# Full 128x128 stationaries for every matmul of the attentions and the decays

## The chip, the cores and the metric

The kernel runs on one core of a Trainium2 chip. The metric is the device time of one execution in microseconds, the median of the runs of the same kernel.

## The reference, cut to what matters

Two transformer blocks are computed one after the other on a sequence of 256 positions of width 1024, in float32. Three parts matter here.

The first block has a stick-breaking attention with 8 heads of 64 columns. For the scores z = q.k/8 of one head, a strictly causal mask, and s before t, the weight is sigmoid(z[t,s]) times the product of (1 - sigmoid(z[t,j])) over s < j < t. The output is the weights times the values.

The second block has a gated delta rule with 8 heads of 128 columns in chunks of 64 positions. It needs two masked matrices of decays exp(G[c] - G[s]) for each head, one with the diagonal and one without, multiplied into the products q.k and k.k.

Beside it stands a forgetting attention, a causal softmax attention with 8 heads of 128 columns, to whose scores cum[t] - cum[s] is added, where cum is the running sum of the log forget gates.

## The kernel before, in words

Positions are split into two tiles of 128. Large projections (`proj_T`, L237) stream their weights from HBM in pieces of 512 KB; ScalarE rounds a piece to f32r (`wh`, L192), VectorE makes the rest (`wl`, L193), and TensorE multiplies the rounded weights with the activation's two halves (L232, 512 columns a pass) and the rests with its upper half (L234, 256 columns). ScalarE and VectorE add the two halves of a result into SBUF (L245, L246). `proj_N512` does the same with positions on the output's partitions (L270 to L272).

The small attention steps are threaded into these projections: generators stand in a list `late`, and `tick()` (called in every column tile of a projection) advances the first of them at a set pace. `piped` runs three heads staggered, each with one of its three steps. The order of instructions on each engine is then worked out by a planner, from priorities and from when operands are expected to be ready; it is not written out by hand.

A matmul's stationary operand is loaded by an instruction of its own (PEld in the profile). An f32 matmul is two passes, an f32r matmul one.

In `att_head` (L500) a mask is laid into a PSUM bank by an identity times `mstrict` (L505, 384 columns: two triangles with zeros between them), and the scores are added: L506 and L507 have 64 rows of `kT` as their stationary, since a head is 64 partitions of a tile that holds two heads. The second step multiplies by triangles of minus ones (L518, L519). The third multiplies the weights with 64 columns of the values `vN` (L525, L526) into 64 partitions of the bank.

In `gdn_products` (L906) each head gets a mask by an identity times `mgdn` (L914, 512 columns), and the sums of the log decays by a matmul whose stationary is a column of `selc` repeated, on 40 rows (L915); the rows `o.rows` hold the sums of 8 heads at partitions 0 to 7 and the rests of their rounding at 32 to 39. Then come the products of queries and keys (L922, L923).

In `fox_head` (L1097) it is the same with `mfox` (L1101), the rows `frows` on 40 partitions (L1102), and the scores (L1105), which have full stationaries, as have the values of this attention (L1130, L1131).

The masks are built on GpSimd at the start of the program. The delta rule's substitution runs on GpSimd later (L935 to L952), beside the projections of the forgetting attention, and its results are loaded by L962 for the matmuls from L971 on.

Of the kernel before, what the change touches and what calls it, by code (L numbers as in the profile page):

```python
# [11 lines left out]
F32 = mybir.dt.float32  # L12
# [6 lines left out]
P = 128  # L19
# [20 lines left out]
def two_blocks(ctx, tc, ins, out):  # L40
# [16 lines left out]
    def nm(s):  # L57
        cnt[0] += 1
        return f"{s}_{cnt[0]}"

    def t4(s, shape=(P, 4, T), dt=F32):
        return p4.tile(list(shape), dt, tag="t4", name=nm(s))
# [73 lines left out]
    def sel(dst, op, fill, base, cm, pattern):  # L136
        nc.gpsimd.affine_select(out=dst, in_=dst, compare_op=op, fill=fill, base=base,
                                pattern=pattern, channel_multiplier=cm)
# [305 lines left out]
        mm_N(pv[tt], wrow[k], k, h, k, tt, slice(None), k == 0, k == KD - 1)  # L444
    for tt in range(NT):
        nc.scalar.copy(vN[:, tt, :], pv[tt])
    qT, kT = t4("qT"), t4("kT")
    for j, pt in proj_T(w_in, 0, ATT_W, h):
        nc.scalar.activation(qT[:, j:j + 2, :], pt, AF.Copy, scale=HEAD_DIM ** -0.5)
    for _ in proj_T(w_in, ATT_W, ATT_W, h, into([kT])):  # L450
        pass

# [9 lines left out]

    mtmp = t2("mtmp")

    mstrict = const.tile([P, 384], F32R, tag="mstrict", name="mstrict")
    nc.gpsimd.memset(mtmp, 0.0)
    sel(mtmp[:, 0:128], ALU.is_gt, -BIG, 0, -1, [[1, P]])
    sel(mtmp[:, 256:384], ALU.is_gt, -BIG, 0, -1, [[1, P]])
    nc.gpsimd.tensor_copy(mstrict, mtmp[:, 0:384])
    def row_tile(n, tag):  # L470
        return t1(tag, (n, P))

# [28 lines left out]
    def att_head(hp, hh):  # L501
        hd = 2 * hp + hh
        rows = slice(hh * 64, (hh + 1) * 64)
        pz = ps("pz")
        mm(pz[:, 0:384], ident_r, mstrict, start=True, stop=True)  # L505
        mm(pz[:, 0:256], kT[rows, hp, 0:P], qT[rows, hp, :], start=False, stop=True, skip_group_check=True)  # L506
        mm(pz[:, 256:384], kT[rows, hp, P:T], qT[rows, hp, P:T], start=False, stop=True, skip_group_check=True)  # L507
        la = ta("la")
        nc.scalar.activation(la[:, 0:384], pz[:, 0:384], AF.Abs)
        nc.scalar.activation(la[:, 0:384], la[:, 0:384], AF.Exp, scale=-1.0)  # L510
        nc.scalar.activation(la[:, 0:384], la[:, 0:384], AF.Ln, bias=1.0)
        nc.vector.scalar_tensor_tensor(la[:, 0:384], pz[:, 0:384], 0.0, la[:, 0:384], ALU.max, ALU.add)
        sr = tc4("sr", (P, 2, 512), F32R)
        nc.scalar.copy(sr[:, 0, 0:384], la[:, 0:384])
        nc.vector.tensor_tensor(sr[:, 1, 0:384], la[:, 0:384], sr[:, 0, 0:384], op=ALU.subtract)
        yield
        for q in range(2):
            mm(pz[:, 0:384], nsuf_r, sr[:, q, 0:384], start=False, stop=True, skip_group_check=True)  # L518
            mm(pz[:, P:T], nones_r, sr[:, q, 256:384], start=False, stop=True, skip_group_check=True)  # L519
        wgt = la  # L520
        nc.scalar.activation(wgt[:, 0:384], pz[:, 0:384], AF.Exp)
        yield
        cs = slice(hd * 64, (hd + 1) * 64)
        po = pz[rows, 0:T]
        mm(po, vN[:, 0, cs], wgt[:, 0:256], start=True, stop=True)  # L525
        mm(po[:, P:T], vN[:, 1, cs], wgt[:, 256:384], start=False, stop=True, skip_group_check=True)  # L526
        hi, lo = oh.at(hp)
        split(hi[rows], lo[rows], po)

    def piped(gens):  # L530

# [23 lines left out]


    mtmp2 = t2("mtmp2")
    mfox = const.tile([P, 384], F32R, tag="mfox", name="mfox")
    nc.gpsimd.memset(mtmp2, 0.0)
    sel(mtmp2[:, 0:128], ALU.is_ge, -BIG, 0, 1, [[-1, P]])  # L560
    sel(mtmp2[:, 256:384], ALU.is_ge, -BIG, 0, 1, [[-1, P]])
    nc.gpsimd.tensor_copy(mfox, mtmp2[:, 0:384])

    mtmp3 = t2("mtmp3")
    mgdn = const.tile([P, 512], F32R, tag="mgdn", name="mgdn")
    nc.gpsimd.memset(mtmp3, 0.0)
    for a in range(4):
        o = a * P
        sel(mtmp3[:, o:o + P], ALU.is_ge if a < 2 else ALU.is_gt, -BIG, 0, -1, [[1, P]])
    nc.gpsimd.tensor_copy(mgdn, mtmp3)  # L570
    zero = const.tile([P, 160], F32, tag="zero", name="zero")
    nc.gpsimd.memset(zero, 0.0)

    selt = const.tile([40, 8], F32, tag="selt", name="selt")
    nc.gpsimd.memset(selt, 0.0)
    for q in (0, 32):
        nc.gpsimd.memset(selt[q:q + 8], 1.0)
        sel(selt[q:q + 8], ALU.is_equal, 0.0, 0, 1, [[-1, 8]])
    selc = const.tile([40, 8], F32R, tag="selc", name="selc")
    nc.gpsimd.tensor_copy(selc, selt)  # L580

    bias24 = const.tile([P, 24], F32, tag="bias24", name="bias24")
# [192 lines left out]
    def gate_sums():  # L775

        pG = ps("pG")
        pGt = pG[:, 0:80].rearrange("p (t c) -> p t c", t=NT)
        mm(pGt[:, :, 24:32], ctr, vals[:, :, 0:8], start=True, stop=True)
        mm(pGt[:, :, 32:40], suf, vals[:, :, 0:8], start=True, stop=True)  # L780
        mm(pGt[:, :, 0:24], tri, vals, start=True, stop=True)
        mm(pGt[:, 1, 16:24], ones, vals[:, 0, 16:24], start=False, stop=True, skip_group_check=True)
        nc.vector.tensor_copy(Gs, pGt)
        nc.vector.tensor_scalar(sl2, Gs[:, :, 16:24], -1.0, None, ALU.mult)
        nc.scalar.activation(beta, vals[:, :, 8:16], AF.Exp)
        nc.scalar.activation(eG, Gs[:, :, 0:8], AF.Exp)
        nc.vector.tensor_scalar(hbeta, beta, 0.5, None, ALU.mult)
        pr_ = to_rows(sl2[:, :, None, :])

        frows = const.tile([40, 384], F32R, tag="frows", name="frows")  # L790
        nc.vector.tensor_copy(frows[:, 0:P], pr_[:, 0, 0:P])
        nc.vector.tensor_copy(frows[:, P:384], pr_[:, 0])
        return frows

    def sum_sq(dst, y):

# [87 lines left out]
    def gdn_decay(o):  # L884

        h0 = o.h0

        ln = tn("ln", (P, HG, NT))
        nc.scalar.activation(ln, o.sk, AF.Ln, bias=eps4)
        nc.vector.tensor_scalar(ln, ln, -0.5, None, ALU.mult)  # L890
        G, Gc, Gr = (Gs[:, :, k + h0:k + h0 + HG].rearrange("p t h -> p h t") for k in (0, 24, 32))
        lb = vals[:, :, 8 + h0:8 + h0 + HG].rearrange("p t h -> p h t")

        rv = tn("rv", (P, NT, 2, HG))
        rvv = rv.rearrange("p t a h -> p a h t")
        o.cv = pg1.tile([P, 3, HG, NT], F32, tag="cv", name=nm("cv"))
        nc.vector.tensor_add(o.cv[:, 1], ln, lb)
        nc.vector.tensor_copy(rvv[:, 0], Gc)
        nc.vector.tensor_add(rvv[:, 1], o.cv[:, 1], Gc)
        o.rows = p1.tile([40, 2, T], F32R, tag="rows", name=nm("rows"), bufs=1)  # L900
        nc.vector.tensor_copy(o.rows, to_rows(rv))

        nc.vector.tensor_sub(o.cv[:, 0], ln, Gc)
        nc.vector.tensor_add(o.cv[:, 1], o.cv[:, 1], G)
        nc.vector.tensor_add(o.cv[:, 2], ln, Gr)
        nc.scalar.activation(o.cv[:, 1:3], o.cv[:, 1:3], AF.Exp)  # L906

    def gdn_products(o):

        M = tc4("M", (P, HG, NT, P))  # L910
        o.At = tc4("At", (P, HG, NT, P))
        for hl in range(HG):
            pd = ps("pd", (P, 2, NT, P))
            mm(pd, ident_r, mgdn, start=True, stop=True)  # L914
            mm(pd, selc[:, hl:hl + 1].to_broadcast([40, P]), o.rows, start=False, stop=True, skip_group_check=True)  # L915
            ed = ta("ed", (P, 2, NT, P))
            for tt in range(NT):
                nc.scalar.activation(ed[:, :, tt, :], pd[:, :, tt, :], AF.Exp, bias=o.cv[:, 0, hl, tt:tt + 1])
            pk = ps("pk", (P, 2, NT, P))
            for tt in range(NT):  # L920
                xs = slice(tt * P, (tt + 1) * P)
                mm(pk[:, 0, tt, :], o.kT[:, hl, xs], o.qT[:, hl, xs], start=True, stop=True)  # L922
                mm(pk[:, 1, tt, :], o.kT[:, hl, xs], o.kT[:, hl, xs], start=True, stop=True)  # L923
            nc.vector.tensor_mul(M[:, hl], pk[:, 1], ed[:, 1])
            nc.vector.tensor_mul(o.At[:, hl], pk[:, 0], ed[:, 0])

        o.Mu = M.rearrange("p h t c -> p (h t) c")
        for b in range(4):
            bs = slice(b * 32, (b + 1) * 32)
            nc.sync.dma_start(scr[o.hg * UN:(o.hg + 1) * UN, b].rearrange("u r c -> r u c"), o.Mu[bs, :, bs])  # L930
# [166 lines left out]
    def fox_head(n, hl, qkT):  # L1097
        hd = n * HG + hl
        fq, fk = qkT[0][:, hl, :], qkT[1][:, hl, :]
        pz = ps("pz")  # L1100
        mm(pz[:, 0:384], ident_r, mfox, start=True, stop=True)  # L1101
        mm(pz[:, 0:384], selc[:, hd:hd + 1].to_broadcast([40, P]), frows, start=False, stop=True,  # L1102
           skip_group_check=True)
        for o, m, q0 in ((0, 1, 0), (128, 2, P)):
            mm(pz[:, o:o + m * P], fq[:, q0:q0 + P], fk[:, 0:m * P], start=False, stop=True,  # L1105
               skip_group_check=True)
# [37 lines left out]
                rests.pop(0)()  # L1144

    steps(gdn_k(g_[0]), 3)
    frows = gate_sums()
    steps(gdn_q(g_[0]), 3)
    g_.append(gdn_open(1))
    rests.append(lambda: gdn_decay(g_[0]))  # L1150
# [120 lines left out]
```

## Time and profile before

| what | value |
|---|---|
| median of 3 runs | 928.37 us (927.98 to 928.56) |
| profiled execution | 928.64 us, span 926.9 us |
| TensorE matmuls busy | 910.3 us (98%), 4891 |
| weight loads busy | 763.9 us (82%) |
| VectorE busy | 656.6 us (71%) |
| ScalarE busy | 571.5 us (62%) |
| GpSimd busy | 73.1 us (8%) |
| granted TensorE clock, mean | 0.998 of full speed |
| HBM read | 154.11 MB |

The span runs from the first to the last instruction of the profiled execution. Matmuls are pipelined and the ends of their records are modelled, so that a busy TensorE need not be at its peak; what a matmul adds to the end is better read in the chain of waits, where each piece reaches from the end of the piece before it to its own.

### The profile page before, as it was taken

The page shows a single profiled execution, that of the slowest core. Times are in us where ns is not written, and L with a number is a line of the kernel's source. Part 1 is how long each engine was busy: PE and PEld are TensorE (multiplying, and loading weights), DVE is VectorE, ACT ScalarE, POOL GpSimd, SP SyncE. Part 2 cuts the span into 40 slices and gives each one's busy share as a digit, 9 for nine tenths or more (in the row PEclk, how much of TensorE's full clock was granted, in tenths as well). Part 3 has the DMA queues.
Part 4 walks back from the last instruction along what each step waited for, and adds up shares of the span by engine and source line. Part 5 has one row for each costly group of instructions (what it writes and reads, how often), then busy time and mean ns, then how long its engine had stood idle before and what let it go on. Part 6 is the DMA issues. An engine that isn't in the chain of part 4 may idle for free.

```text
span 926.9 us, 13384 instructions
## 1 busy us (share of the span) xinstructions
PE 910.3 (98%) x4891; PEld 763.9 (82%) x4891; DVE 656.6 (71%) x1154; ACT 571.5 (62%) x990; POOL 73.1 (8%) x127
## 2 busy tenths in 40 slices
PE   8999999999999999999999999999999999999998
PEld 4887888778888888778888768888998788888886
DVE  6556656985988889857989878645688765555553
ACT  5567765565765666647867667754455466556662
POOL 4000000000000000000000189401000000000000
PEclk9999999999999999999999999999999999999999
DMA  7653457556565555663645344544336754556552
GB/s 251 198 171 94 137 173 236 168 184 218 178 207 168 191 187 193 206 192 118 200 138 151 106 130 141 166 138 128 112 120 234 261 168 150 188 176 197 173 168 99
DMA packets 118873, 157.86 MB, mean 170 GB/s; under 512 B 9829, under 2 KB 96088, under 8 KB 118808
## 3 DMA queue, kind: packets, MB, share of 16 engines
q1 hardware_dynamic: 117336, 153.08, 51.7%
q10 hardware_dynamic: 720, 2.62, 0.9%
q0 software_dynamic: 752, 1.31, 0.6%
q8 instruction: 38, 0.62, 0.3%
q14 instruction: 27, 0.22, 0.1%
HBM read 154.11 MB, written 2.88 MB: 169 GB/s over the span
## 4 chain that ended last, share of the span: by engine, by line
PE 82%; DVE 8%; DMA 5%; ACT 3%; issue 2%; SPq 0%; ACTq 0%; DVEq 0%
PE pT L232 30%; PE pT L234 15%; PE pN L271 5%; PE pN L270 5%; PE pN L272 5%; PE pM L270 4%; PE pM L271 4%; PE pM L272 4%; DVE wl L193 3%; PE pS L1006 2%; DMA raw<-in_w_out_dram 1%; ACT wh L192 1%; DMA raw<-in_w_down_dram 1%; DMA raw<-in_w_up_dram 1%; DMA raw<-in_w_in_dram 1%
## 5 line engine op out<-in xcount | busy, mean ns | idle before, releaser
L193 DVE TENSOR_TENSOR wl<-raw,wh 128x1024 fp32r<-128x1024 f32 (+1 forms) x283 | 346.3, 1231 | 98.7 <-PE pT L234 74.0
L192 ACT CAST wh<-raw 128x1024 fp32r<-128x1024 f32 (+1 forms) x283 | 290.7, 1047 | 101.4 <-PE pT L232 38.0
L232 PE MATMUL pT<-uT,wh 128*128 128x512 f32 x384 | 102.2, 402 | 0.0
L246 DVE TENSOR_TENSOR py<-py,pT 128x256 f32<-128x256 f32 x136 | 56.0, 417 | 54.5 <-ACT py L245 54.1
L245 ACT COPY py<-pT 128x256 f32<-128x256 f32 x136 | 49.0, 369 | 60.2 <-PE pT L234 59.9
L270 PE MATMUL pN<-wh,fTh 128*128 128x512 f32 x216 | 84.1, 393 | 0.8 <-ACT wh L192 0.5
L271 PE MATMUL pN<-wl,fTh 128*128 128x512 f32 x216 | 84.2, 391 | 0.1
L272 PE MATMUL pN<-wh,fTl 128*128 128x512 f32 x216 | 83.8, 390 | 0.0
L232 PEld LDWEIGHTS pT<-uT,wh 128*128 128x128 f32 x384 | 68.5, 189 | 12.6 <-issue 0.5
L232 PE MATMUL pT<-hT,wh 128*128 128x512 f32 x288 | 73.4, 396 | 0.0
L232 PE MATMUL pT<-h2T,wh 128*128 128x512 f32 x288 | 72.2, 392 | 0.0
L232 PEld LDWEIGHTS pT<-hT,wh 128*128 128x128 f32 x288 | 51.6, 189 | 10.4 <-issue 0.2
L232 PEld LDWEIGHTS pT<-h2T,wh 128*128 128x128 f32 x288 | 52.1, 189 | 9.6
L234 PEld LDWEIGHTS pT<-uT,wl 128*128 128x128 f32 x384 | 52.3, 190 | 3.6
L234 PE MATMUL pT<-uT,wl 128*128 128x256 f32 x384 | 53.8, 283 | 0.0
L270 PEld LDWEIGHTS pN<-wh,fTh 128*128 128x128 f32 x216 | 40.5, 188 | 9.6 <-ACT wh L192 1.2
L232 PE MATMUL pT<-hnT,wh 128*128 128x512 f32 x192 | 47.8, 391 | 0.0
L271 PEld LDWEIGHTS pN<-wl,fTh 128*128 128x128 f32 x216 | 40.6, 188 | 8.4 <-DVE wl L193 0.5
L272 PEld LDWEIGHTS pN<-wh,fTl 128*128 128x128 f32 x216 | 40.6, 188 | 8.5
L234 PEld LDWEIGHTS pT<-hT,wl 128*128 128x128 f32 x288 | 39.3, 190 | 2.9
L234 PEld LDWEIGHTS pT<-h2T,wl 128*128 128x128 f32 x288 | 39.3, 190 | 2.8
L935 POOL DMA_DIRECT2D bm<-scr x1 | 0.8, 775 | 515.1 <-PE pM L271 515.1
(380 smaller groups left out, 1647.0 us busy)
## 6 DMA issues: line engine op xcount, KB each, us to landing
raw<-in_w_in_dram SPq DMA_DIRECT2D x111, 512.0 KB, 3.9
raw<-in_w_up_dram SPq DMA_DIRECT2D x76, 512.0 KB, 4.6
raw<-in_w_down_dram SPq DMA_DIRECT2D x54, 512.0 KB, 4.3
raw<-in_w_out_dram SPq DMA_DIRECT2D x16, 512.0 KB, 4.1
raw<-in_w_proj_fox_dram SPq DMA_DIRECT2D x8, 512.0 KB, 3.5
raw<-in_w_proj_gdn_dram SPq DMA_DIRECT2D x8, 512.0 KB, 4.2
raw<-in_w_att_branch_dram SPq DMA_DIRECT2D x4, 512.0 KB, 5.0
raw<-in_w_conv_branch_dram SPq DMA_DIRECT2D x4, 512.0 KB, 4.1
```

The source lines that it names most:

```text
L192: nc.scalar.copy(wh, raw)
L193: nc.vector.tensor_sub(wl, raw, wh)
L232: mm(dst, wt.at(k, cs)[0], x.both(k), start=(k == 0), stop=(k == kt - 1), skip_group_check=True)
L234: mm(dst[:, T:2 * T], wt.at(k, cs)[1], x.at(k)[0], start=False, stop=(k == kt - 1), skip_group_check=True)
L245: nc.scalar.copy(y[:, i, :], pt[:, 0:T])
L246: nc.vector.tensor_add(y[:, i, :], y[:, i, :], pt[:, T:2 * T])
L270: mm(dst, xh, wh, start=first, stop=False)
L271: mm(dst, xh, wl, start=False, stop=False)
L272: mm(dst, xl, wh, start=False, stop=last)
L935: nc.gpsimd.dma_start(bm, scr.rearrange("u b r c -> (u b) r c"))
L1006: mm(pt[:, hl, :], *f(hl), start=True, stop=True)
```

## The change

Every matmul of these three parts gets a stationary of 128 rows and 128 columns. The scaled queries of the first attention go into tiles in which the other head's 64 rows are zero, so that all 128 rows of `kT` can be the stationary. Its values are multiplied for both heads at once, and the half that belongs to the head is read out. The rows of sums (`grows`, `frows`) and `selc` are extended from 40 to 128 partitions with zeros; the two groups of heads share `grows`. The masks hold one triangle each, which the moving operand repeats (`diagonal`); where the mask was zero, nothing is written. In a forgetting head the rows of sums now come first and the mask second.

```diff
-    qT, kT = t4("qT"), t4("kT")
+    qz, kT = [tc4("qz", (P, 2, 2, T)) for _ in range(2)], t4("kT")
+    for q_ in qz:
+        for hh in range(2):
+            nc.gpsimd.memset(q_[(1 - hh) * 64:(2 - hh) * 64, :, hh, :], 0.0)
     for j, pt in proj_T(w_in, 0, ATT_W, h):
-        nc.scalar.activation(qT[:, j:j + 2, :], pt, AF.Copy, scale=HEAD_DIM ** -0.5)
+        for hh in range(2):
+            rows = slice(hh * 64, (hh + 1) * 64)
+            nc.scalar.activation(qz[j // 2][rows, :, hh, :], pt[rows], AF.Copy, scale=HEAD_DIM ** -0.5)
...
-    mstrict = const.tile([P, 384], F32R, tag="mstrict", name="mstrict")
+    mstrict = const.tile([P, P], F32R, tag="mstrict", name="mstrict")
...
+    def diagonal(pz, mask, start):
+
+        mm(pz.rearrange("p (b c) -> p b c", b=2)[:, :, 0:P], ident_r, mask[:, None, :].to_broadcast([P, 2, P]),
+           start=start, stop=True, skip_group_check=True)
...
-        mm(pz[:, 0:384], ident_r, mstrict, start=True, stop=True)
-        mm(pz[:, 0:256], kT[rows, hp, 0:P], qT[rows, hp, :], start=False, stop=True, skip_group_check=True)
-        mm(pz[:, 256:384], kT[rows, hp, P:T], qT[rows, hp, P:T], start=False, stop=True, skip_group_check=True)
+        q_ = qz[hp // 2][:, hp % 2, hh, :]
+        diagonal(pz, mstrict, True)
+        mm(pz[:, 0:256], kT[:, hp, 0:P], q_, start=False, stop=True, skip_group_check=True)
+        mm(pz[:, 256:384], kT[:, hp, P:T], q_[:, P:T], start=False, stop=True, skip_group_check=True)
...
-        cs = slice(hd * 64, (hd + 1) * 64)
-        po = pz[rows, 0:T]
+        cs = slice(hp * P, (hp + 1) * P)
+        po = pz[:, 0:T]
         mm(po, vN[:, 0, cs], wgt[:, 0:256], start=True, stop=True)
         mm(po[:, P:T], vN[:, 1, cs], wgt[:, 256:384], start=False, stop=True, skip_group_check=True)
         hi, lo = oh.at(hp)
-        split(hi[rows], lo[rows], po)
+        split(hi[rows], lo[rows], po[rows])
...
+    grows = const.tile([P, 2, T], F32R, tag="grows", name="grows")
+    nc.gpsimd.tensor_copy(grows.rearrange("p a t -> p (a t)"), mtmp2)
+    frows = const.tile([P, 384], F32R, tag="frows", name="frows")
+    nc.gpsimd.tensor_copy(frows, mtmp2[:, 0:384])
...
-    mgdn = const.tile([P, 512], F32R, tag="mgdn", name="mgdn")
+    mgdn = const.tile([P, 2, P], F32R, tag="mgdn", name="mgdn")
...
-    selc = const.tile([40, 8], F32R, tag="selc", name="selc")
+    selc = const.tile([P, 8], F32R, tag="selc", name="selc")
...
-        o.rows = p1.tile([40, 2, T], F32R, tag="rows", name=nm("rows"), bufs=1)
-        nc.vector.tensor_copy(o.rows, to_rows(rv))
+        nc.vector.tensor_copy(grows[0:40], to_rows(rv))
...
-            mm(pd, ident_r, mgdn, start=True, stop=True)
-            mm(pd, selc[:, hl:hl + 1].to_broadcast([40, P]), o.rows, start=False, stop=True, skip_group_check=True)
+            mm(pd, ident_r, mgdn[:, :, None, :].to_broadcast([P, 2, NT, P]), start=True, stop=True)
+            mm(pd, selc[:, hl:hl + 1].to_broadcast([P, P]), grows, start=False, stop=True, skip_group_check=True)
...
-        mm(pz[:, 0:384], ident_r, mfox, start=True, stop=True)
-        mm(pz[:, 0:384], selc[:, hd:hd + 1].to_broadcast([40, P]), frows, start=False, stop=True,
-           skip_group_check=True)
+        mm(pz[:, 0:384], selc[:, hd:hd + 1].to_broadcast([P, P]), frows, start=True, stop=True)
+        diagonal(pz, mfox, False)
```

## Rows read from the trace of the kernel before

**Rows 1.** The page's chain of waits, summed by engine.

```profile
PE 82%; DVE 8%; DMA 5%; ACT 3%; issue 2%; SPq 0%; ACTq 0%; DVEq 0%
```

**Rows 2.** Busy us per engine in three stretches (PE, PEld, DVE, ACT, POOL), clock, DMA, GB/s.

```profile
49.00:120.00 71.00, 71.00 (x382) 57.67 (x381) 46.78 (x78) 51.18 (x93) 0.00 (x0) 1.00 0.42 128
476.00:523.00 47.00, 47.00 (x260) 38.04 (x259) 41.61 (x99) 33.51 (x74) 0.00 (x0) 1.00 0.37 115
540.00:563.00 23.00, 21.14 (x98) 15.78 (x96) 18.30 (x39) 15.62 (x44) 20.96 (x27) 1.00 0.40 122
```

**Rows 3.** The chain in order of time, stick-breaking heads: start us, us added, piece.

```profile
56.52 0.18 PE pz L518
...
57.27 0.63 PE pz L506 x2
57.89 0.22 PE pz L507 x2
58.11 2.05 PE pT L232 x8
...
61.11 1.84 PE pT L232 x8
...
63.90 0.58 PE pz L525 x2
...
64.70 0.37 PE pz L518
...
80.37 0.41 PE pz L507 x2
```

**Rows 4.** Timeline of TensorE, first forgetting head: start us, us, engine, line, operation, shapes.

```profile
540.56 0.39 PE L272 MATMUL pM<-wh,uT 128*128 128x512 f32 x1
540.57 0.19 PEld L1101 LDWEIGHTS pz<-mfox,ident_r 128*128 128x128 f32 x1
...
540.79 0.34 PE L1101 MATMUL pz<-mfox,ident_r 128*128 128x384 f32 x1
...
541.05 0.18 PEld L1102 LDWEIGHTS pz<-frows,selc 40*128 40x128 f32 x1 [0.30 <-issue]
```

**Rows 5.** The chain in order of time, forgetting heads.

```profile
557.75 0.17 PE pz L1101
557.92 0.36 PE pz L1102
...
558.65 0.66 PE pz L1105 x4
...
566.37 0.43 PE pz L1130 x2
...
586.10 0.85 PE pz L1105 x4
```

**Rows 6.** The chain in order of time, decays of the delta rule.

```profile
483.80 0.24 PE pd L914
484.03 0.43 PE pd L915
...
486.90 0.42 PE pk L922 x2
...
487.55 0.22 PE pk L922 x2
```

**Rows 7.** The chain in order of time, where the substitution's result is first used.

```profile
606.70 0.84 PE pY L971 x8
```

**Rows 8.** Line 449: duration of one in ns (shortest, median, longest), starts, shapes.

```profile
L449 ACT ACTIVATE qT<-py x2: 632/633/634, 33.5 to 39.1; 128x512 f32<-128x512 f32 x2
```

**Rows 9.** The chain in order of time, ahead of the first forgetting head's maximum.

```profile
540.77 2.77 DVE wl L193 x2
```

**Rows 10.** Timeline of GpSimd, loads of the substitution's result.

```profile
590.41 2.30 POOL L962 DMA_DIRECT2D X<-scT  x4 [0.29 <-POOL X L959]
```

**Rows 11.** The chain in order of time, at the branch projections.

```profile
146.06 5.57 DMA raw<-in_w_att_branch_dram
```

More of the change, by code (lines that the diff above doesn't have):

```diff
@@ L463, in two_blocks @@
     mtmp = t2("mtmp")
-    mstrict = const.tile([P, 384], F32R, tag="mstrict", name="mstrict")
[L466 to L469, printed above, removed]
+    mstrict = const.tile([P, P], F32R, tag="mstrict", name="mstrict")
+    nc.gpsimd.memset(mtmp[:, 0:P], 0.0)
+    sel(mtmp[:, 0:P], ALU.is_gt, -BIG, 0, -1, [[1, P]])
+    nc.gpsimd.tensor_copy(mstrict, mtmp[:, 0:P])
+    def diagonal(pz, mask, start):
+        mm(pz.rearrange("p (b c) -> p b c", b=2)[:, :, 0:P], ident_r, mask[:, None, :].to_broadcast([P, 2, P]),
+           start=start, stop=True, skip_group_check=True)
     def row_tile(n, tag):
@@ L557, in two_blocks @@
     mtmp2 = t2("mtmp2")
-    mfox = const.tile([P, 384], F32R, tag="mfox", name="mfox")
+    mfox = const.tile([P, P], F32R, tag="mfox", name="mfox")
     nc.gpsimd.memset(mtmp2, 0.0)
-    sel(mtmp2[:, 0:128], ALU.is_ge, -BIG, 0, 1, [[-1, P]])
-    sel(mtmp2[:, 256:384], ALU.is_ge, -BIG, 0, 1, [[-1, P]])
-    nc.gpsimd.tensor_copy(mfox, mtmp2[:, 0:384])
-    mtmp3 = t2("mtmp3")
-    mgdn = const.tile([P, 512], F32R, tag="mgdn", name="mgdn")
[L566 to L570, printed above, removed]
+    grows = const.tile([P, 2, T], F32R, tag="grows", name="grows")
+    nc.gpsimd.tensor_copy(grows.rearrange("p a t -> p (a t)"), mtmp2)
+    frows = const.tile([P, 384], F32R, tag="frows", name="frows")
+    nc.gpsimd.tensor_copy(frows, mtmp2[:, 0:384])
+    sel(mtmp2[:, 0:P], ALU.is_ge, -BIG, 0, 1, [[-1, P]])
+    nc.gpsimd.tensor_copy(mfox, mtmp2[:, 0:P])
+    mtmp3 = t2("mtmp3")
+    mgdn = const.tile([P, 2, P], F32R, tag="mgdn", name="mgdn")
+    nc.gpsimd.memset(mtmp3[:, 0:2 * P], 0.0)
+    for a in range(2):
+        sel(mtmp3[:, a * P:(a + 1) * P], ALU.is_gt if a else ALU.is_ge, -BIG, 0, -1, [[1, P]])
+    nc.gpsimd.tensor_copy(mgdn.rearrange("p a c -> p (a c)"), mtmp3[:, 0:2 * P])
     zero = const.tile([P, 160], F32, tag="zero", name="zero")
     nc.gpsimd.memset(zero, 0.0)
-    selt = const.tile([40, 8], F32, tag="selt", name="selt")
+    selt = const.tile([P, 8], F32, tag="selt", name="selt")
     nc.gpsimd.memset(selt, 0.0)
@@ L788, in gate_sums @@
         pr_ = to_rows(sl2[:, :, None, :])
[L790 to L793, printed above, removed]
+        nc.vector.tensor_copy(frows[0:40, 0:P], pr_[:, 0, 0:P])
+        nc.vector.tensor_copy(frows[0:40, P:384], pr_[:, 0])
     def sum_sq(dst, y):
@@ L1146, in two_blocks @@
     steps(gdn_k(g_[0]), 3)
-    frows = gate_sums()
+    gate_sums()
     steps(gdn_q(g_[0]), 3)
```

## The prediction

> **What bounds the kernel now.** First I read the chain of waits, summed by engine [rows 1]: TensorE holds 82% of it, VectorE 8%, the DMAs 5%. So time taken off TensorE is worth something where the chain runs on TensorE, and nothing where it runs elsewhere; the question has to be asked stage by stage. Next come the busy times of the stretches with edited matmuls [rows 2]. In 49 to 120 us (the stick-breaking heads, threaded into projections) TensorE is busy in every microsecond, VectorE 46.78 of 71.00 and ScalarE 51.18: room on both. In 476 to 523 (the decays of the delta rule) TensorE is again always busy, but VectorE is at 41.61 of 47.00, with 5.4 us left. In 540 to 563 (the first four forgetting heads) TensorE rests for 1.9 us of 23 and the chain runs on other engines.
>
> Then the chain in order of time, piece by piece; its second column is what each piece adds to the end. The reader is to compare equal work. A 384-column pass on a full stationary adds 0.18 us (L518), but 0.37 right after the 64-column stationaries of L525 and L526. Eight passes of a projection add 1.84, but 2.05 right after L507, whose stationary has 64 rows [rows 3]. Nothing is late there: the two columns of TensorE's instructions show why [rows 4]. The load of a full stationary (L1101) starts 0.01 us after the matmul ahead of it started and lies wholly beside it; the load of the 40-row one (L1102) starts 0.26 us after L1101's matmul did, with 0.30 us of idle loader ended by "issue", which is nobody's result. A change of the stationary's shape costs a pause, both going in and coming out.
>
> **The change part by part.** Everything is summed against the profiled execution, 928.64 us (span 926.9), which is 0.27 above the median of the three runs.
>
> *Stick-breaking, in.* The two passes of L506 add 0.63 us [rows 3]; two 256-column passes of a full f32 stationary, L1130, add 0.43 [rows 5]. So 0.20 a head, 8 heads: 1.6. The zero rows themselves cost nothing: columns set the length of a pass, and their number stays. *Out*, into a projection: 2.05 - 1.84 = 0.21, 8 times, with smaller ones among them: 1.6. In two heads other matmuls stand between L506 and L507, so that L507 pays its own way in (0.41 against 0.22 [rows 3]) and the matmul between pays a way out (0.20): 2 x 0.39 = 0.8.
>
> *Values.* L525's two passes add 0.58 against the 0.43 of L1130: 0.15, 8 times, 1.2. The way out, 0.37 - 0.18 = 0.19, 8 times: 1.5. Both heads' values make the stationary 128 columns wide, L1130's shape exactly. Sum for this attention: 1.6 + 1.6 + 0.8 + 1.2 + 1.5 = 6.7.
>
> *Decays.* L915 adds 0.43 where 512 columns on a full stationary, L914, add 0.24: 0.19. The pair of passes behind it adds 0.42 where the next pair adds 0.22: 0.20 [rows 6]. 8 x 0.39 = 3.1.
>
> *Forgetting heads.* L1102 adds 0.36 where L1101 with as many columns adds 0.17; the four passes of L1105 add 0.85 behind it and 0.66 where a full stationary comes first [rows 5]. 8 x 0.38 = 3.0.
>
> *Masks.* One triangle in two places is 256 columns and not 384. By L1101, 0.17 us for 384, the 128 saved are 0.057 us, in 16 heads 0.9. The repeated reading and the gap in the output are new; L971 reads and writes short strided pieces, eight passes in 0.84 us or 0.105 each [rows 7], no more than the 0.11 of a pass in L922's quick pair [rows 6], so I charge nothing and bound it by a loss of 0.1 us in each of 24 mask matmuls (2.4 us).
>
> *Moved and added work.* The scaled queries are written by four ScalarE instructions of 64 partitions and not two of 128. One of 128x512 takes 632 ns [rows 8]; if half the partitions take as long, ScalarE has 1.3 us more between 33 and 39 us, beside TensorE's projections; uncovered it is a loss of 1.3, if halves take half, none. GpSimd gains four fills and two copies and loses mask work, all of it before the heads need it. The order of the mask and the row matmul in a forgetting head is swapped, with one end. No DMA and no wait is added. Total taken off TensorE: 6.7 + 3.1 + 3.0 + 0.9 = 13.7 us.
>
> **What of it lies on the path.** The stick-breaking part, 6.7 + 0.45 = 7.15, all of it: TensorE is the chain from 49 to 120 and the other engines have 20 us of room [rows 2]. Of the decays, between 0 and 3.1: VectorE has 5.4 us of rest in that stretch, but it is spread, and its work follows TensorE's; I take 2.3, three quarters, nearest to the row that has the chain on TensorE throughout. Of the first four forgetting heads, between 0 and 1.75 (4 x 0.38 + 4 x 0.057): at 540.77 the chain leaves TensorE for 2.77 us of VectorE's weight conversion [rows 9], and TensorE has rest already [rows 2], so I take 0; VectorE and ScalarE are late next there. The last four heads are on a chain of TensorE pieces (the 0.85 of [rows 5] is one): 1.75. GpSimd's substitution does not become late: its last load is issued from 590.41 [rows 10], and what needs it starts at 606.70 [rows 7], while only the 3.5 us of the forgetting heads come off between. Forecast: 7.15 + 2.3 + 0 + 1.75 = 11.2; 928.64 - 11.2 = 917.4, and by the median 917.2. I say 917.2, with 915.9 to 918.7 as this case's own range.
>
> A rule of the Trainium skill speaks against the change: in "TensorE: Matmul & The Clock Gate", section "Part 3: Packing small matmuls", a weight load overlaps a running matmul only where their row groups differ. By it a full stationary could never load beside another, and the sum would turn into the loss of the last rival below; by the rows it does load beside one, and the sum stands.
>
> **The rivals.** *All of it is on the path.* If VectorE's queue keeps up in both doubtful stretches, 928.64 - 13.7 = 914.9. For it: the 5.4 us of rest. Against: the rest of TensorE in 540 to 563.
>
> *VectorE becomes the bound* from the decays to the first forgetting heads, and what TensorE saves there turns into its waiting for converted weights: 928.64 - 7.15 - 1.75 = 919.7. For it: VectorE at 41.61 of 47.00 and the handover at 540.77. Against: up to there no piece of the chain is VectorE's.
>
> *The first gain is given back* at 146.06, where the chain passes for 5.57 us through the DMA of the branch weights [rows 11]: if that stream can't come sooner, 7.15 is lost and 928.64 - 4.05 = 924.6 stays. Against: the DMAs are at 0.42 of their time in 49 to 120 [rows 2], and a load is issued when TensorE and the converters free a buffer, so it moves with them.
>
> *It doesn't do what it says:* the pauses belong to the switch between f32 and f32r, or to a first use of an operand, and stay. Then only the masks count: 928.64 - 0.9 = 927.7. Against: L1130 and the 0.66 of L1105 are f32 passes behind f32r or transposes, with no pause [rows 5].
>
> *Slower.* Full loads are exposed. The change makes 80 loads full (32 for the scores, 32 for the values, 16 rows of sums). If each stood in line with the passes for its 0.19 us [rows 4], that would be 15.2, and 928.64 - 11.2 + 15.2 = 932.6. It decides from 0.14 us a load on. Against: the load of L1101 beside a running matmul [rows 4]. The page named above has the mechanism; the trace disagrees with it for full stationaries.
>
> **How the numbers follow.** Forecast 50%; all on the path 15%; VectorE the bound 20%; given back 8%; pauses stay 4%; slower 3%. The first three hold 85%, and the unknown prices (1.3 for ScalarE, 2.4 for the masks' access) reach a little beyond 919.7: range 913.5 to 922. The order of instructions on each engine is worked out anew for a changed kernel, which may move a stage by a microsecond either way; the range has room for it. A difference under 0.2% (1.9 us) can't be told from none: faster 0.93, same 0.04, slower 0.03.
>
> **What would show it.** In the profile after: no "issue" idle ahead of the score, value and row-sum loads; L506's successor at 0.43 for two passes, the value passes likewise; eight projection passes behind them at 1.84; the decay's row matmul at 0.24 and the pair behind it at 0.22; masks at 0.11 to 0.12. The stretch of the stick-breaking heads should end some 7 us sooner, and TensorE's rest after the decays should grow by 1 to 3 us. Wrong would be: loads that start after their matmuls and not beside them; a chain that runs on VectorE in the decays; the 7 us present at 120 and gone by 200.

## The result and the profile after

The changed kernel takes 918.36 us (median of 4 runs, 916.61 to 919.42), the kernel before 928.17 in 4 runs beside it: the ratio is 0.9898, with a 95% interval of 0.9879 to 0.9918. The forecast was 917.2. 9.8 us came off where 11.2 were forecast. That it came so near is in part luck: by the table of stages below, 4.55 us of losses that were not forecast stand against 2.73 of gains that were not forecast either. The profiled execution took 919.42 us, its span 917.7.

The edited matmuls have new line numbers: in the stick-breaking heads the mask is L478, the scores L518 and L519, the suffix triangles L530 and L531, the values L538 and L539; in the decays the mask is L927, the rows L928, the products L935 and L936; in the forgetting heads the rows are L1114, the mask L478 again, the scores L1117.

First the page: busy time by engine, and the chain summed by engine (against [rows 1]).

```profile
PE 899.6 (98%) x4891; PEld 763.2 (83%) x4891; DVE 656.4 (72%) x1154; ACT 572.6 (62%) x992; POOL 74.1 (8%) x129
...
PE 80%; DVE 10%; ACT 3%; DMA 3%; issue 2%; POOL 1%; DVEq 0%; ACTq 0%; SPq 0%; POOLq 0%
```

TensorE still holds the chain, with 2 points fewer and VectorE with 2 more. Next the same three stretches of work as in [rows 2], cut where the trace of after starts and ends the same matmuls: busy us of PE, PEld, DVE, ACT and POOL, clock, DMA share, GB/s.

```profile
48.50:113.80 65.30, 65.01 (x382) 57.16 (x381) 46.17 (x78) 51.30 (x93) 0.00 (x0) 1.00 0.46 138
472.40:516.50 44.10, 44.10 (x260) 38.20 (x259) 41.15 (x98) 33.22 (x74) 0.00 (x0) 1.00 0.43 123
533.40:555.60 22.20, 19.59 (x100) 15.67 (x98) 17.89 (x39) 15.63 (x44) 20.24 (x26) 1.00 0.44 127
```

The 382 matmuls of the first stretch take 65.30 us where they took 71.00, and TensorE now has small rests among them (0.29 us). The decays still show none. Then the chain in order of time in the stick-breaking heads, start us, us added, piece (against [rows 3]).

```profile
62.53 0.43 PE pz L538 x2
...
63.19 0.17 PE pz L530
...
63.71 0.17 PE pz L478
63.88 0.43 PE pz L518 x2
...
64.53 1.85 PE pT L232 x8
```

Values 0.43 (before 0.58), scores 0.43 (0.63), the projection behind them 1.85 (2.05), the triangle behind the values 0.17 (0.37): each pause is gone. The timeline of the first forgetting head shows how (against [rows 4]).

```profile
533.95 0.39 PE L272 MATMUL pM<-wh,uT 128*128 128x512 f32 x1
533.95 0.19 PEld L1114 LDWEIGHTS pz<-frows,selc 128*128 128x128 f32 x1
...
534.17 0.33 PE L1114 MATMUL pz<-frows,selc 128*128 128x384 f32 x1
534.17 0.19 PEld L478 LDWEIGHTS pz<-mfox,ident_r 128*128 128x128 f32 x1
```

The load of the row matmul, late by 0.26 us when it had 40 rows, starts with the matmul ahead of it. The decays and the forgetting heads, chain in order of time (against [rows 6] and [rows 5]):

```profile
477.65 0.23 PE pd L927
477.89 0.23 PE pd L928
...
478.58 0.22 PE pk L935 x2
...
578.04 0.17 PE pz L1114
578.21 0.12 PE pz L478
578.33 0.66 PE pz L1117 x4
```

Rows 0.23 for 0.43, the first pair behind them 0.22 for 0.42, rows of a forgetting head 0.17 for 0.36, its scores 0.66 for 0.85.

**Where the time came from, stage by stage.** I take the start of the same matmul in two traces, named by its time in before, and subtract what the stage started with. Minus is a gain, in us.

| from, to (us of before) | forecast | after | after, again | gain loads moved |
|---|---|---|---|---|
| start to 26.7 | 0 | -0.47 | -1.94 | -0.86 |
| to 137.6, stick-breaking | -7.15 | -5.73 | -5.74 | -5.76 |
| to 211.3, branches, merge, norms | 0 | +2.62 | +1.06 | -0.87 |
| to 476.3 | 0 | +0.04 | -0.09 | +0.01 |
| to 529.7, decays | -2.3 | -3.00 | -3.03 | -3.04 |
| to 563.1, first four forgetting heads | 0 | -0.98 | -0.62 | -0.90 |
| to 606.5, last four | -1.75 | -1.28 | -0.70 | -1.28 |
| to 765.7 | 0 | -0.58 | -0.40 | -0.59 |

The columns behind "after" are experiments 5 and 6. The first stage has no part of the change; over all profiles it differs by up to 2.7 us, so its figure is left out of the readings. Two stages ask for a reason: the stick-breaking heads gave 1.4 less than forecast, and the stage behind them gave 2.62 back. For the first, the chain of after a little later shows who comes last, and the waits of TensorE's loader between 40 and 130 us show how often (engine, line, releaser: us in total, times, longest).

```profile
71.73 0.69 DVE cu L609
...
75.76 0.52 ACT sr L526
...
76.30 0.57 DVE sr L527
...
76.92 0.45 PE pz L530
```

```profile
PEld pz L530 <- ACT sr L526: 1.0, 2, 0.6
PEld pz L530 <- DVE sr L527: 0.6, 2, 0.3
```

In the middle heads the convolution branch's product (L609) and taps share VectorE with the head's logarithm part `sr`, and with TensorE faster `sr` is late: 0.45 for a triangle that takes 0.17 above. Some 20 us later the chain pays for two more:

```profile
97.58 0.39 PE pz L530
...
98.55 0.26 PE pz L530
```

For the second, ScalarE's waits between 134 and 160 us, and the issue and landing of the load it waited for, first in after and then in before.

```profile
ACT wh L192 <- DMA raw<-in_w_conv_branch_dram: 3.4, 1, 3.4
```

```profile
L176 SPq DMA_DIRECT2D raw<-in_w_conv_branch_dram x1: 368/368/368, 136.0 to 136.0; - x1
...
DMA to landing us min/median/max: 9.5/9.5/9.5
```

```profile
L176 SPq DMA_DIRECT2D raw<-in_w_conv_branch_dram x1: 368/368/368, 141.9 to 141.9; - x1
...
DMA to landing us min/median/max: 6.2/6.2/6.2
```

The branch weight is issued 5.9 us sooner than before, but lands in 9.5 us where it took 6.2. Right behind it, on ScalarE's queue, go the two gain loads of the coming norms (512 KB each), issued at 136.3 and 136.7 in after, 142.5 and 142.9 before. What the late weight passes on is seen further down the chain: VectorE's conversions (`wl`, L193) come later, so the buffer that the first piece of the next weight, `in_w_out`, is to fill comes free later, and the chain goes through that load, first in after and then in before.

```profile
150.18 1.15 DVE wl L193
...
151.38 4.70 DMA raw<-in_w_out_dram
```

```profile
156.17 4.33 DMA raw<-in_w_out_dram
```

Counted from the start of the last gate projection (131.40 in after, 137.60 in before), this load is issued 1.41 us later than before and takes 0.37 longer.

### The profile page after: what moved, and what is told of

It is laid out like the page before. It is cut to its first block, busy times and chain, and to the rows that moved or that the text cites. A ratio compares the mean times of both kernels' runs of the same rounds, so it can differ in the third digit from the quotient of the medians.

```text
span 917.7 us, 13382 instructions
## 1 busy us (share of the span) xinstructions
PE 899.6 (98%) x4891; PEld 763.2 (83%) x4891; DVE 656.4 (72%) x1154; ACT 572.6 (62%) x992; POOL 74.1 (8%) x129
## 3 DMA queue, kind: packets, MB, share of 16 engines
q10 hardware_dynamic: 720, 2.62, 0.9%
## 4 chain that ended last, share of the span: by engine, by line
PE 80%; DVE 10%; ACT 3%; DMA 3%; issue 2%; POOL 1%; DVEq 0%; ACTq 0%; SPq 0%; POOLq 0%
PE pT L232 29%; PE pT L234 15%; PE pN L270 5%; PE pN L271 5%; PE pN L272 5%; DVE wl L193 5%; PE pM L271 4%; PE pM L272 4%; PE pM L270 4%; PE pS L1019 2%; ACT wh L192 1%; DMA raw<-in_w_up_dram 1%; DMA raw<-in_w_out_dram 1%; DMA raw<-in_w_in_dram 1%; DVE py L246 1%
## 5 line engine op out<-in xcount | busy, mean ns | idle before, releaser
L193 DVE TENSOR_TENSOR wl<-raw,wh 128x1024 fp32r<-128x1024 f32 (+1 forms) x283 | 346.7, 1232 | 95.9 <-PE pT L234 71.0
L272 PE MATMUL pN<-wh,fTl 128*128 128x512 f32 x216 | 83.8, 390 | 0.0
L272 PEld LDWEIGHTS pN<-wh,fTl 128*128 128x128 f32 x216 | 40.6, 188 | 8.5
```

The source lines that it names most:

```text
L193: nc.vector.tensor_sub(wl, raw, wh)
L272: mm(dst, xl, wh, start=False, stop=last)
```

## The experiments

Four kernels make one part of the change each, two pairs test the stage that gave back, and three ask what else the pauses and waits allow. None leaves out part of the computation.

**1. Scores alone** (zero-filled queries, full stationary; values, rows and masks as before).

```
-        mm(pz[:, 0:256], kT[rows, hp, 0:P], qT[rows, hp, :], start=False, stop=True, skip_group_check=True)
...
+        q_ = qz[hp // 2][:, hp % 2, hh, :]
+        mm(pz[:, 0:256], kT[:, hp, 0:P], q_, start=False, stop=True, skip_group_check=True)
```

> The kernel before with one part of the change: the scores of the stick-breaking heads with zero rows beside the 64, nothing else. Theory (a pause of 0.2 us at each change of the stationary's shape): two 256-column score passes add 0.43 and not 0.63 us, the projection passes behind them 1.84 and not 2.05; by 120 us the trace is 3.2 to 4.0 us ahead of before; the total is 2 to 4 us lower, less what is given back between 155 and 205 us. Rival (the pause belongs to the switch between f32 and f32r): no row changes, total within 1 us.

Measured: 924.77 us (8 runs) to 927.34 (20), ratio 0.9968 [0.9954, 0.9982]. The stick-breaking stage gained 3.79 of the 4.0 of the forecast's terms; 0.71 was given back by 211 us. Its chain (values are L531, scores L512):

```profile
62.46 0.58 PE pz L531 x2
...
64.21 0.43 PE pz L512 x2
...
64.86 1.82 PE pT L232 x8
```

The scores and the projection behind them lose their pauses, the values keep theirs: a pause goes with the shape of its own stationary.

**2. Values alone.**

```
-        cs = slice(hd * 64, (hd + 1) * 64)
-        po = pz[rows, 0:T]
+        cs = slice(hp * P, (hp + 1) * P)
+        po = pz[:, 0:T]
```

> The kernel before with the values of both heads as a 128-column stationary, nothing else. Theory: value passes 0.43 for two and not 0.58, the pass behind them 0.17 and not 0.37; 2.4 to 2.8 us ahead by 120 us; total 1 to 3 us lower. Rival (a column width costs nothing, since stationaries of 40 and 24 columns show no pause in the trace of before): rows and total as before.

Measured: 923.99 (7 runs), ratio 0.9968 [0.9955, 0.9981]. The stage gained 2.90 (terms: 2.7), and 1.90 was given back by 211 us. The chain is the mirror of the last one (values L525, scores L506):

```profile
61.27 0.43 PE pz L525 x2
...
62.67 0.63 PE pz L506 x2
...
63.52 2.05 PE pT L232 x8
```

**3. Row sums alone** (decays and forgetting heads).

```
-            mm(pd, selc[:, hl:hl + 1].to_broadcast([40, P]), o.rows, ...)
+            mm(pd, selc[:, hl:hl + 1].to_broadcast([P, P]), grows, ...)
```

> The kernel before with the sums' rows and their selector on 128 partitions instead of 40, masks as they were. Theory: the row matmuls of the decays add 0.23 and not 0.42 us and those of the forgetting heads 0.17 and not 0.36, the passes behind them 0.2 less; 6 us off TensorE, of which 4.5 to 5.5 show in the total, since in the whole change the decays gave 3.05 and the forgetting heads 2.2 with their masks. Rival (VectorE bounds the decays): under 2 us.

Measured: 923.01 (4 runs), ratio 0.9951 [0.9936, 0.9966]. Nothing in the stick-breaking stage (-0.01), 3.05 in the decays, 2.06 in the forgetting heads.

```profile
482.33 0.24 PE pd L915
482.57 0.23 PE pd L916
```

The decays' sum of 3.1 comes in full, so VectorE doesn't bound that stretch.

**4. Masks alone.**

```
-        mm(pz[:, 0:384], ident_r, mstrict, start=True, stop=True)
+        diagonal(pz, mstrict, True)
```

> The kernel before with masks of one triangle, repeated by the moving operand, and all stationaries of 64 and 40 as before (in the forgetting heads the 40-row matmul comes first). Theory: the 16 masks of the attentions lose 0.05 us each, those of the decays nothing, pauses all stay: 0.5 to 1 us off TensorE, total lower by 0 to 1 us, no difference that can be measured. Rival (the masks carry a good part of the gain): 3 us or more lower. Second rival (the repeated reading or the gap in the output is slow): mask matmuls longer than before.

Measured: 925.49 (10 runs), ratio 0.9980 [0.9969, 0.9991], which is 1.85 us by medians and more than was expected; the stages show 0.50 in the stick-breaking heads and 0.92 in the forgetting ones, 1.4 together. The pauses stay:

```profile
62.55 0.17 PE pz L471
62.72 0.63 PE pz L510 x2
```

By stage, the parts gain 3.79 + 2.90 + 0.50 = 7.19 in the stick-breaking heads, the forecast's 7.15; together they gain 5.73.

**5 to 7. The changed kernel again, the changed kernel with the two gain loads earlier, and the kernel before with them earlier.** The loads move from behind the last gate projection to its inside, some 11 us ahead; nothing else changes.

```
         for j, pt in proj_T(w_in, CB + 3 * CONV_W + gi * D, D, h, into(s)):
             nc.scalar.activation(pt, pt, AF.Sigmoid)
+            if gi == 1 and j == 0:
+                g_post = gain_bc("norm_mix_post")
+            if gi == 1 and j == 2:
+                g_pre = gain_bc("norm_ffn_pre")
...
-    g_post = gain_bc("norm_mix_post")
-    g_pre = gain_bc("norm_ffn_pre")
```

> The changed kernel as it is, beside the three others on one chip. Theory: ratio to before 0.988 to 0.992 as measured; in its trace the first piece of the second pair of branch weights (issued some 0.3 us ahead of the two gain vectors' loads) lands 6 to 10 us after issue, and of the 5.7 us won by 150 us between 1.5 and 3 are gone by 211. Rival (the give-back was one execution's accident): under 1 us is gone.

> The changed kernel with the two 512 KB loads of the gain vectors issued some 20 us earlier, inside the last gate projection, and not at the head of the branch projections. Theory (the 2.6 us given back between 150 and 211 us are branch weights landing late beside these loads): the weights land in 5 to 6 us, ScalarE no longer waits 3.4 us for them, at 211 us the trace keeps 1.5 to 3 us more of the gain, total 1.5 to 3 us below the changed kernel. Rival (VectorE's own queue bounds the branch projections): landing earlier changes nothing, same total.

> The kernel before with the same move of the two gain loads. Theory: its branch weights landed in 6.2 us and ScalarE waited less for them (1.7 us), so it wins less than the changed kernel does, 0 to 1.5 us. Rival: no difference in either kernel.

Measured, to 926.45 for before (13 runs): again 917.33, ratio 0.9902 [0.9888, 0.9917]; with the loads moved 915.09, 0.9878 [0.9863, 0.9893]; before with them moved 925.49 (10 runs), 0.9992 [0.9982, 1.0002]. So the move brings 2.24 us by medians in the changed kernel, and nothing that can be told from none in the one before. ScalarE's waits between 134 and 160 us with the loads moved no longer name the convolution branch's weight:

```profile
ACT wh L192 <- DMA raw<-in_w_in_dram: 3.3, 1, 3.3
```

That wait comes ahead of any need of TensorE's and costs nothing. The next table follows the lateness through all the kernels, counted from the start of the last gate projection, in us against before. "Third" is the conversion of the third piece of the branch weights, the one that waited for the late load (149.02 us in before, 145.57 in after); "out" is the conversion of the first piece of `in_w_out` (160.51 and 156.10); the last column is what is given back between 137.6 and 168.9 us.

```
kernel            third late   out late   given back by 168.9
rows alone            0.00      -0.35          -0.04
before, moved         0.00      -1.14          -0.04
after, moved          0.00      -1.37          -0.04
moved again (11)      0.00      -1.25          -0.04
GpSimd (exp. 10)      0.00      -0.94          -0.04
masks alone           0.10       0.28           0.27
scores alone          0.53       0.55           0.56
values alone          0.76       1.07           1.06
inverse (exp. 8)      1.37       1.38           1.36
after, again          1.51       0.82           0.82
edge (exp. 9)         1.62       0.19           0.21
after                 2.76       1.79           1.79
```

Wherever the third conversion is late, something is given back, but not in step with it: 1.62 us late cost 0.21 in experiment 9, 1.37 cost 1.36 in experiment 8. What is given back equals the lateness of the first `in_w_out` piece, within 0.03 us in every kernel in which that piece is late. With the gain loads moved, the branch weight is no longer waited for and the `in_w_out` piece comes sooner than in before.

The remaining 0.83 of the 2.62 (168.9 to 211.3 us) lies in a stretch that differs by as much without the change: rows alone, which changes nothing up to there, loses 0.88 in it, and the kernels range from a gain of 1.09 to that loss. Three of the four kernels with the loads moved gain 0.83 to 1.09 there, before with them moved among them, so that a part of the 2.24 us may come from here. What the move shows is that the loads' place makes the weight late. Why it takes 9.5 us beside them and 6.2 before, where they follow as closely, stays open.

**8. Another small matmul made full:** 64x64 stationaries with 64 columns, 16 passes in the delta rule's inverse.

```
-            mm(pU[lo, u_, :], W[hi, 0, u_, :], X[hi, u_, hi], start=True, stop=True)
+            mm(pU[:, u_, :], XT[:, u_, :], X[:, u_, hi], start=True, stop=True)
```

> The changed kernel with one more group of matmuls on full stationaries: the last step of the delta rule's inverse (stationary 64x64 before, 128x128 now, 64 moving columns, 16 passes, twice). Theory: a pass of 64 columns on a full stationary takes the time of the load, 0.105 us, and not 0.058; 16 passes cost 1.68 us against 1.07, and 0.2 comes back behind them: about 0.4 us longer each time, 0.8 in all, none that the total can show. Rival (a full stationary always wins): 0.4 us shorter each time.

Measured: 918.41, ratio 0.9916 [0.9901, 0.9931]; from 606.5 to 648.5 us it loses 0.85 us against before, where after gains 0.05. The group in this kernel, then in after:

```profile
614.21 1.73 PE pU L1006 x16
615.94 0.98 PE pT L232 x4
```

```profile
615.63 1.07 PE pU L1006 x16
616.70 1.14 PE pT L232 x4
```

The way out is gone (0.98 for 1.14), but the 16 passes take 0.108 us each and not 0.067: the loader has no rest among them, and a full load (0.19 us) starts only every 0.11 us, a 64x64 one (0.13 us) every 0.058 in after. Net 0.50 slower each time.

**9. Where the pause begins.** A pass of 256 columns (L539), its result overwritten, ahead of the full value passes (L540), with another stationary in each head. No part of the output depends on it; one run, 924.4 us, whose time means nothing here.

```
+        r, n = [(P, 72), (P, 64), (P, 40), (P, 96), (72, P), (64, P), (40, P), (96, P)][hd]
+        mm(pz[0:n, 0:T], vN[0:r, 0, hp * P:hp * P + n], wgt[0:r, 0:256], start=True, stop=True)
```

> The changed kernel with one probe in each stick-breaking head, ahead of its value matmuls, which overwrite it: an f32 matmul of 256 columns (two passes) whose stationary has, in heads 0 to 7: 72, 64, 40 and 96 columns on 128 rows; 72, 64, 40 and 96 rows with 128 columns. A probe without a pause adds 0.43 us and the two value passes behind it 0.43. Theory: from 65 to 128 rows or columns there is no pause; 64 columns, 64 rows and 40 rows pause (0.15 to 0.20 in and 0.20 out); 40 columns do not, as 40 and 24 columns did not in the trace of before. Rival (anything but 128x128 pauses): seven of eight... all eight probes pause.

The chain in order of time: 72 columns, 40 columns, 64 rows.

```profile
61.57 0.43 PE pz L539 x2
62.00 0.43 PE pz L540 x2
...
75.15 0.56 PE pz L539 x2
75.71 0.63 PE pz L540 x2
...
96.75 0.63 PE pz L539 x2
97.38 0.63 PE pz L540 x2
```

72 and 96, rows or columns, cost nothing (0.43 and 0.43 each); 64 (0.58 and 0.63 for columns, 0.63 and 0.63 for rows) and 40 (0.56 and 0.63, 0.63 and 0.63) pay on the way in and out. The expectation that 40 columns wouldn't pause was wrong. It came from 40-column loads of f32r data, whose loader sits idle 0.0 us in before; this one is f32, and whether that is the difference wasn't tried.

**10 and 11. The product on GpSimd,** to take load off VectorE where `sr` is late, with the gain loads moved; and experiment 6 again beside it.

```
-        nc.vector.tensor_mul(cu[:, j:j + 2, :], pt, cc[:, j:j + 2, :])
+        nc.gpsimd.tensor_mul(cu[:, j:j + 2, :], pt, cc[:, j:j + 2, :])
```

> The changed kernel with the gain loads issued earlier and, besides, the two products of the convolution's inputs (L609, 0.69 us each) on GpSimd instead of VectorE. Theory (the stick-breaking part gave 5.7 and not 7.15 us since VectorE is late for the middle heads, where the convolution falls on it): L530 no longer waits for VectorE near 77 us, the trace is 0.4 to 0.8 us further ahead by 111 us, and the total is 0 to 0.8 us below the kernel with the moved loads alone. Rival (the shortfall is elsewhere): no change by 111 us, total the same.

> The changed kernel with the gain loads issued earlier, once more and on the same chip as the run with the products on GpSimd: 0.986 to 0.990 of before.

Measured, to 927.3 (7 runs): 917.01, ratio 0.9881 [0.9861, 0.9901], and 916.43, 0.9878 [0.9862, 0.9894]. The product on GpSimd isn't better; its stick-breaking stage gained 4.22, not 5.75. Two triangles lose what is missing. The first (at 75.5 us, 0.68 more than in after) stands in the new order of instructions ahead of the next head's mask and scores, which fill its wait in after. The timeline shows the second (at 84.6 us, 0.85 more):

```profile
81.89 2.19 POOL L609 TENSOR_TENSOR cu<-py,cc 128x512 f32<-128x512 f32 x1 [10.22 <-DVE py L246]
...
82.87 1.63 DVE L527 TENSOR_TENSOR sr<-la,sr 128x384 fp32r<-128x384 f32 x1
```

The very instruction that was to come sooner takes 1.63 us beside GpSimd's and 0.56 in after, and GpSimd's takes 2.19 here where its first takes 1.28. That the two engines hold each other up is argued from this overlap and was not tried by itself. So the experiment doesn't tell what an earlier `sr` would be worth. Experiment 6 is ahead of the kernel before in both groups of runs and of the changed one where they ran together (915.09 to 917.33), and is the version to keep.

## Why the prediction was right, and where it wasn't

**The mechanism** held at every place it named: the switch of the stationary's shape costs about 0.2 us in and 0.2 out, it goes when the shape is full, and zero rows cost nothing. Experiments 1 to 4 take the pauses away one by one, so the rival "it doesn't do what it says" fell, and so did the slower one: the full loads lie beside the running matmuls (L1114's beside L272's). The Trainium skill, "TensorEngine Tiling (Array Packing)", section "Key Properties", says that a change of the tiling mode drains TensorE. The rows agree in that what they price at 0.2 us is the change, in and out, and experiment 9 puts 72 and 96 with 128, and 40 with 64; that a drain is what takes this time, no run here shows.

**The stick-breaking sum** (7.15, "all of it") was mis-sized: each part was worth its term (3.79 for 4.0, 2.90 for 2.7, 0.50 for 0.45), and together 5.73. The step that failed is "the other engines have 20 us of room". The room was there over the stretch and not in the middle heads, where `sr` became the late piece: the triangles' loads waited 1.6 us for it in after, and the waits of scores alone and values alone list none for it. What that cost can be read from the matmuls themselves, each from the end of the one before it to its own end: the four late triangles of after (at 76.3, 76.9, 97.6 and 98.6 us) took 0.63, 0.54, 0.39 and 0.26 us, the same four in scores alone 0.17, 0.23, 0.18 and 0.18. That is 1.06 of the missing 1.42. By the same count the other 0.36 lies in the terms, the largest part, about 0.25, in the ways out of the small stationaries. That an earlier `sr` would bring the 1.06 back is not shown, since the attempt to bring it forward failed for other reasons. The terms also overlap: in values alone the order of work has one split head and not two, so that part of the 2 x 0.39 is in its gain as well.

**The gain lasts:** this step failed. I gave the place 8%, with the reason that a load "moves with" TensorE. The load was issued sooner, landed late beside two others, and passed its lateness on to the next weight: 1.79 of 5.73 in after, 0.82 when run again, none with the two loads moved. The rival had nearly the right place and a price far too large. The sign that the prediction named, 7 us present at 120 and gone by 200, came in part: the trace is 6.20 us ahead at 137.6 and 3.58 at 211.3.

**The decays** were too small at 2.3: 3.00 to 3.05 of 3.1 came in every kernel that has them. The caution about VectorE (41.61 of 47.00) was unfounded; its share rose to 41.15 of 44.10 and TensorE still has no rest there.

**The forgetting heads** were 0 + 1.75 and came as 0.98 + 1.28. TensorE's rest in the first four grew from 1.86 to 2.61 us, so part of their saving did turn into rest (0.75 us, where 1 to 3 were named as a sign), but not all; part of the last four's was lost too, and what follows them there was not traced.

**The masks** cost 0.12 in the forgetting heads as said, but 0.17 in the stick-breaking ones, where the suffix passes ahead take 0.06 and the full load of 0.19 can't lie beside so short a pass (that is argued from experiment 8, not tried). The 0.05 saved is what the forecast had. **ScalarE's added instructions** cost nothing visible: from 26.7 to 53.6 us after is 0.46 ahead and not behind.

## What to carry to other kernels

Look in the chain for equal passes of unequal price; where a small stationary stands among full ones, filling it with zeros to 128x128 saves some 0.4 us an episode, as long as its passes have enough columns to cover the load (passes of 256 columns did, passes of 64 didn't). Room on another engine has to be read at the piece that follows, not as a sum over 70 us. When a stage gets shorter, look at what is issued at its end: two transfers that nobody waits for took up to 1.8 us of the gain, and moving them cost nothing. And a wait has to be followed to the piece on the chain: the load that landed late was not the one whose lateness the time showed.

## What the hardware showed that I had not expected

The pause sets in between 64 and 72, the same for rows and for columns (f32 stationaries, experiment 9). A 512 KB load took 9.5 us ahead of two others in after and 6.2 ahead of the same two in before. A VectorE tensor operation of 0.56 us took 1.63 beside a GpSimd one over 128x512, which took 2.19 itself, 1.28 the time before, and 0.69 on VectorE.
